# A hybrid decoder layer: where the last gate tile of the first feed-forward lies, how the norms take their root, and which engines scale the last block

## The chip, the cores and the metric

The kernel runs on one core of a Trainium2 chip. TensorE multiplies matrices (PE in the profile, its weight loads PEld), VectorE (DVE), ScalarE (ACT) and GpSimd (POOL) work on tiles in on-chip memory, SyncE (SP) issues DMA transfers. The metric is the device time of one execution in microseconds; a time stated for a kernel is the median of its runs.

## The reference

One layer of a decoder on 1024 tokens of width 1024, with 16 learned meta tokens in front, all in float32:

```
h = concat(meta, x)
u = rmsnorm(h)                    # y = x * rsqrt(mean(x*x) + 1e-6) * g
proj = u @ w_in                   # latents, queries, keys, values, indexer
A: latent attention, 8 heads:     q = rmsnorm(c_q) @ w_uq, kv = rmsnorm(c_kv) @ w_ukv, rotary part, causal softmax
B: sparse attention, 8 heads:     indexer scores, top 256 keys of each query, rotary softmax attention on them
h = h + concat(A, B) @ w_o
u = rmsnorm(h)
h = h + (silu(u @ w_gate) * (u @ w_up)) @ w_down      # hidden width 2816
out = rmsnorm(h)[16:]
```

Every norm needs, per row, the reciprocal root of a mean of squares; there are five sorts of norm: of the input, of the two latents, before the feed-forward, and at the end.

## The kernel before

Tokens are cut into eight blocks of 128 rows. Blocks 0 to 2 form part A, blocks 3 to 7 part B. In the order of the source: the input norm and projection with the indexer and the top-k search; attention of part A; the output projection of A (`out_proj`), then attention of part B, head by head, eight latent heads and eight sparse ones; the first feed-forward (`ffn`) on A; `out_proj` on B; the second feed-forward (`ffn_sums`), which forms its products from seven sums of quarter blocks; and the last norm (`last_norm`) of each block as soon as its rows are complete. Float32 factors are split into a high and a low half (`split`: ScalarE writes the high half, VectorE or GpSimd the difference, GpSimd in pieces of 256 columns), and each product is three matmuls (`three`, lines 196 to 198).

The order of the instructions on an engine isn't that of the source. The framework (a tile context) is built with `schedule_with_timeline_sim=True`: it places each instruction by its own estimate of durations when the kernel is built, so that work of later stages stands between instructions of earlier ones where memory allows. An engine then takes its queue in that fixed order. A tile's memory is given to the next tile of its name in a pool's ring when all its users are done.

The parts that matter here:

- `rstd` (L151 to L162) turns a column of sums into reciprocal roots: a scaled copy, ScalarE's root, VectorE's reciprocal, then one Newton step in four VectorE instructions (L158 to L161). The input norm calls it for nine row groups, the two latent norms 17 times together (name `rsc`), `out_proj` six times (once for three blocks of A together, once for each block of B), and `last_norm` eight times.
- `attention` (L847) keeps the split keys of a head in one of two pairs of tiles `kT`, used in turn; each holds 128 rows by the number of keys (1040 in part B). They lie in the pool `ab`. A head's scores go through an exponential on ScalarE (L799), a cast on VectorE (L819), a difference on GpSimd (L821) and a transposing DMA into `pT` (L823), then to the values' matmuls (L830 to L832).
- `ffn` (L1127) takes 22 tiles of the hidden width in turn. For each it loads a gate, an up and a down tile into `raw` (two slots in turn), and splits them with GpSimd. Gate and up tiles share a ring of two pairs (`fw`, `WF = 2`), the down tiles have another ring of two (`fu`). When it ends, its pools are closed, and the transposed rows of part B (`us`) are laid over them.
- `out_proj` on B transposes the attention's rows (L1036), writes them split into `us`, multiplies, adds the input rows, and norms each block (L1069 scales into `un`); then the block is transposed again (L1072) and its seven sums are written over `us` (`put`, L1097). The second feed-forward's first product needs the sums of all five blocks.
- `last_norm` (L1278): ScalarE squares each half of a block's rows with a running sum (L1287), the two sums are added (L1292), `rstd` follows, and each half of 512 columns is scaled by root and gain, then stored. For the blocks before the last, VectorE does the first half in one instruction (L1301), and ScalarE and GpSimd the second in two (L1298, L1299); for the last block VectorE does both halves.

Of the kernel before, what the change touches and what calls it, by code (L numbers as in the profile page):

```python
# [11 lines left out]
F32 = mybir.dt.float32  # L12
F32R = mybir.dt.float32r
# [5 lines left out]
AF = mybir.ActivationFunctionType  # L19
OP = mybir.AluOpType  # L20
# [5 lines left out]
D = 1024  # L26
P = 128
NB = T // P
# [5 lines left out]
HEADS = 8  # L34
# [5 lines left out]
NF = 2816 // P  # L40
EPS = 1e-6

NA = 3
BLK_A, BLK_B = tuple(range(NA)), tuple(range(NA, NB))
# [30 lines left out]
CH_A = (2, 2, 2)  # L75
# [5 lines left out]
WS_N, RAW_N = 5, 4  # L81
# [24 lines left out]
def hybrid_layer(ctx, tc, a, out):  # L106
    nc = tc.nc
    V, S, G, PE = nc.vector, nc.scalar, nc.gpsimd, nc.tensor
    ld = nc.sync.dma_start
# [40 lines left out]

    def rstd(pool, ss, n, parts=P, tag="rs"):  # L151

        w = ss.shape[-1]
        v = pool.tile([parts, 4, w], F32, name=tag, bufs=3)
        V.tensor_scalar(v[:, 0], ss, 1.0 / n, EPS, op0=OP.mult, op1=OP.add)
        S.activation(v[:, 1], v[:, 0], AF.Sqrt)
        V.reciprocal(v[:, 1], v[:, 1])
        V.tensor_mul(v[:, 2], v[:, 1], v[:, 1])  # L158
        V.tensor_mul(v[:, 2], v[:, 2], v[:, 0])
        V.tensor_scalar(v[:, 2], v[:, 2], -0.5, 1.5, op0=OP.mult, op1=OP.add)  # L160
        V.tensor_mul(v[:, 3], v[:, 1], v[:, 2])  # L161
        return v[:, 3]  # L162

    def v_scale(pool, i, bound, rest):
# [50 lines left out]
    def fill(n):  # L215


        while live and n > 0:
            n -= 1
            for z in list(live):  # L220
                for _ in range(z[1]):
                    if next(z[0], live) is live:
                        live.remove(z)
                        break
# [435 lines left out]
    oh = [op.tile([P, D], F32, name=f"oh{t}") for t in range(NB)]  # L660
# [186 lines left out]
    def attention(pl, blocks, cfg):  # L847
# [2 lines left out]
        cfg["b1"] = b1  # L850
        nb = len(blocks)
        nk = n_keys(b1)
        kT = cfg.get("kT") or [tuple(pl.tile([P, nk], F32R, name=f"k{x}{i}") for x in "HL") for i in range(2)]

        dma = [b for b in blocks if b not in cfg["by_pe"]]
        if dma:
# [108 lines left out]
        for i, (half, h) in enumerate(heads):  # L965
            passes, v = got.pop(i)
# [157 lines left out]
        w = -(-n // k)  # L1124
        return [(i * w, min(n, (i + 1) * w)) for i in range(k)]

    def ffn(fw, fu, blocks, u, psg, psu, pso, ch):  # L1127

        nt = len(blocks) * P
        ch, nh, nw = ch  # L1130
        hid, wdn = {}, {}
        for f in range(NF):
            ws = []
            for name in ("w_gate", "w_up", "w_down"):
                down = name == "w_down"
                pl, n = (fu, nw) if down else (fw, WF)
                raw = fw.tile([P, D], F32, name="raw", bufs=2)
                if down:
                    ld(raw, a[name][0, f * P:(f + 1) * P, :])
                else:  # L1140
                    ld(raw.rearrange("p (d c) -> p d c", c=P),
                       a[name][0, :, f * P:(f + 1) * P].rearrange("(d p) c -> p d c", p=P))
                h = pl.tile([P, D], F32R, name="wH", bufs=n)
                l = pl.tile([P, D], F32R, name="wL", bufs=n)
                split(h, l, raw, G)
                ws.append((h, l))
            wdn[f] = ws[2]
            hH = fu.tile([P, nt], F32R, name="hH", bufs=nh)
            hL = fu.tile([P, nt], F32R, name="hL", bufs=nh)
            hid[f] = hH, hL  # L1150
            for i0, i1 in block_chunks(len(blocks)):
                sl = slice(i0 * P, i1 * P)
                w = (i1 - i0) * P
                pg, pu = psg()[:, :w], psu()[:, :w]
                for o, (h, l) in ((pg, ws[0]), (pu, ws[1])):
                    for d in range(ND):
                        ds_ = slice(d * P, (d + 1) * P)
                        three(o.rearrange("p (b n) -> p b n", n=P), h[:, ds_], l[:, ds_], u[:, i0:i1, 0, d],
                              u[:, i0:i1, 1, d], d == 0, d == ND - 1)
                        if d % 2:  # L1160
                            yield
                sg = fu.tile([P, 512], F32, name="sg", bufs=1)[:, :w]

                S.activation(sg, pg, AF.Tanh, scale=0.5)
                V.scalar_tensor_tensor(sg, sg, 1.0, pg, op0=OP.add, op1=OP.mult)
                V.scalar_tensor_tensor(sg, sg, 0.5, pu, op0=OP.mult, op1=OP.mult)
                split(hH[:, sl], hL[:, sl], sg)
            if (NF - 1 - f) % ch:
                continue
            fs = range(max(0, f - ch + 1), f + 1)  # L1170
            for i, t in enumerate(blocks):
                sl = slice(i * P, (i + 1) * P)
                for c in range(2):
                    cs = slice(c * 512, (c + 1) * 512)
                    po = pso()
                    for g in fs:
                        three(po, hid[g][0][:, sl], hid[g][1][:, sl], wdn[g][0][:, cs], wdn[g][1][:, cs],
                              g == fs[0], g == fs[-1])
                    V.tensor_add(oh[t][:, cs], po, oh[t][:, cs])  # L1179
                    yield  # L1180
# [97 lines left out]
    def last_norm(fu):  # L1278

        gl = fu.tile([P, D], F32, name="gl")  # L1280
        ld(gl, bcast_rows(a["final_norm_g"], D))
        sums = {}

        def half(t, c):
            if not c:
                sums[t] = fu.tile([P, 2], F32, name="ss3", bufs=3)
            S.activation(fu.tile([P, 512], BF, name="yj"), oh[t][:, c * 512:(c + 1) * 512], AF.Square,  # L1287
                         accum_out=sums[t][:, c:c + 1])
            if not c:
                return  # L1290
            tot = fu.tile([P, 1], F32, name="ss4", bufs=3)
            V.tensor_add(tot, sums[t][:, 0:1], sums[t][:, 1:2])  # L1292
            r = rstd(fu, tot, D, P, "rs3")
            for k in range(2):
                y = oh[t][:, k * 512:(k + 1) * 512]
                g = gl[:, k * 512:(k + 1) * 512]
                if k and t < NB - 1:
                    S.activation(y, y, AF.Copy, scale=r)  # L1298
                    G.tensor_mul(y, y, g)  # L1299
                else:  # L1300
                    V.scalar_tensor_tensor(y, y, r, g, op0=OP.mult, op1=OP.mult)  # L1301
                ld(out[0, t * P:(t + 1) * P, k * 512:(k + 1) * 512], y)

        return half
# [8 lines left out]
    cfg = dict(CFG_A, s=ps_s, t=ps_t, o=ps_o, ck=(ckH, ckL), wk=(wkH, wkL), sel=selb, kT=kT_a, q_rows=q_a, v_rows=v_a)  # L1313
    woa = ExitStack()
    with aa_es:
        work = attention(aa, BLK_A, cfg)
        rest = mla_rest()
        n = 0
# [21 lines left out]
    ua = u_tile(pool(ua_es, "ua", side="right"), BLK_A, "ua")  # L1340
    ab = ExitStack()
    pl = pool(ab, "ab", side="right")
    ps_s, ps_t, ps_o, ps_g, ps_u, ps_y = (ring(x) for x in PSB)
# [16 lines left out]
    fw = pool(fa, "fw")  # L1360
    fu = pool(fa, "fua")
    for _ in work:
        fill(1)
    fill(1000)
    ab.close()
    for _ in ffn(fw, fu, BLK_A, ua, ps_g, ps_u, ps_y, CH_A):
        pass
    fa.close()
    ua_es.close()
    us = [pool(ctx, f"us{k}").tile([P, NSEG, 2, 4, SEG], F32R, name=f"us{k}") for k in range(NPR)]  # L1370
# [62 lines left out]
```

## Time and profile before

| | us |
|---|---|
| median of 3 runs | 1507.58 (1507.29 to 1510.57) |
| the profiled execution | 1510.57 |
| its span in the trace | 1508.8 |
| TensorE busy | 1403.7 (93%) |
| VectorE busy | 1101.3 (73%) |
| ScalarE busy | 923.7 (61%) |
| GpSimd busy | 893.6 (59%) |

The span runs from the first to the last instruction in the trace; the rest of an execution's time lies outside it. Busy time is the sum of an engine's instructions; matmuls are pipelined, so a busy TensorE can still be below its peak. Where a row names what ended an engine's idle time, that is inferred from the semaphores.

### The profile page before, as it was taken

How to read it: one execution, taken by the hardware profiler on the slowest of the kernel's cores; microseconds unless marked ns; L12 is line 12 of the kernel's file. 1: busy time of each engine (PE TensorE's matmuls, PEld its weight loads, DVE VectorE, ACT ScalarE, POOL GpSimd, SP SyncE). 2: the span in 40 equal slices, each digit the busy share in tenths (PEclk: the TensorE clock that was granted, in tenths of full speed). 3: DMA queues.
4: the chain of work that ended last, by engine and by line, in shares of the span. 5: the costliest groups of instructions: out<-in, count | busy, mean ns of one | idle time of the engine just before them, and what ended most of it. 6: DMA issues, size and time to landing. Idle time of an engine off the chain costs nothing. (4 is left out here: it accounts for less than half of the span.)

```text
span 1508.8 us, 29965 instructions
## 1 busy us (share of the span) xinstructions
PE 1403.7 (93%) x10320; PEld 1293.0 (86%) x10320; DVE 1101.3 (73%) x2714; ACT 923.7 (61%) x2264; POOL 893.6 (59%) x1185
## 2 busy tenths in 40 slices
PE   6999998899989799899999999897899999999996
PEld 5999998897879689798888888797899999999995
DVE  5888989948886785966776657647566777777766
ACT  5666678896888889788644444554544444444434
POOL 2573555212405587787878879663846666666653
PEclk9999999999999799999999999998899999999998
DMA  6213365223434788678879998661212222222211
GB/s 172 61 48 87 80 139 133 51 89 115 137 113 114 144 187 174 149 154 182 188 162 199 200 214 193 161 189 39 71 57 84 84 84 84 84 75 80 84 56 70
DMA packets 353737, 180.74 MB, mean 120 GB/s; under 512 B 196560, under 2 KB 341344, under 8 KB 353584
## 3 DMA queue, kind: packets, MB, share of 16 engines
q1 hardware_dynamic: 353584, 178.82, 48.0%
q8 instruction: 81, 1.33, 0.4%
q14 instruction: 72, 0.59, 0.1%
HBM read 120.77 MB, written 21.30 MB: 94 GB/s over the span
## 5 line engine op out<-in xcount | busy, mean ns | idle before, releaser
L191 POOL TENSOR_TENSOR wL<-raw,wH 128x256 fp32r<-128x256 f32 x352 | 286.7, 848 | 60.6 <-ACT wH L188 56.3
L821 POOL TENSOR_TENSOR hl<-pd,hl 128x260 f16<-128x260 f32 (+5 forms) x256 | 168.8, 689 | 70.5 <-ACT hl L817 38.0
L191 POOL TENSOR_TENSOR wsl<-raw,wsh 128x256 fp32r<-128x256 f32 x132 | 120.6, 942 | 95.9 <-ACT wsh L188 48.5
L196 PE MATMUL b<-wh,uH 128*128 128x256 f32 (+3 forms) x568 | 169.3, 298 | 5.1 <-DVE mlo L318 3.2
L198 PE MATMUL b<-wh,uL 128*128 128x256 f32 (+3 forms) x568 | 168.8, 298 | 0.0
L197 PE MATMUL b<-wl,uH 128*128 128x256 f32 (+3 forms) x568 | 168.5, 297 | 0.1
L188 ACT ACTIVATE wH<-raw 128x1024 fp32r<-128x1024 f32 x88 | 91.8, 1055 | 80.8 <-DMA raw<-in_w_gate 20.8
L196 PE MATMUL b<-us,wsh 128*128 128x320 f32 x440 | 136.2, 313 | 1.6 <-ACT us L188 1.0
L197 PE MATMUL b<-us,wsh 128*128 128x320 f32 x440 | 136.5, 311 | 0.4 <-DVE us L193 0.4
L198 PE MATMUL b<-us,wsl 128*128 128x320 f32 x440 | 134.8, 310 | 0.0
L196 PE MATMUL b<-ua,wH 128*128 128x384 f32 x352 | 121.8, 346 | 3.3 <-ACT wH L188 3.3
L382 ACT ACTIVATE js<-sc,bs 128x528 bf16<-128x528 int16 (+7 forms) x128 | 120.9, 944 | 4.8 <-DVE sc L437 2.4
L197 PE MATMUL b<-ua,wH 128*128 128x384 f32 x352 | 121.2, 344 | 0.0
L198 PE MATMUL b<-ua,wL 128*128 128x384 f32 x352 | 121.0, 345 | 0.0
L196 PE MATMUL b<-wH,hH 128*128 128x512 f32 x282 | 113.9, 404 | 4.4 <-ACT hH L188 3.1
L196 PEld LDWEIGHTS b<-wh,uH 128*128 128x128 f32 x568 | 108.8, 192 | 7.2 <-DVE mlo L318 3.9
L197 PE MATMUL b<-wL,hH 128*128 128x512 f32 x282 | 112.5, 399 | 0.0
L198 PE MATMUL b<-wH,hL 128*128 128x512 f32 x282 | 110.2, 400 | 0.4 <-DVE hL L193 0.4
L197 PEld LDWEIGHTS b<-wl,uH 128*128 128x128 f32 x568 | 109.1, 192 | 0.5 <-DVE wl L193 0.3
L198 PEld LDWEIGHTS b<-wh,uL 128*128 128x128 f32 x568 | 109.0, 192 | 0.4 <-DVE uL L193 0.2
L1248 DVE TENSOR_TENSOR oh<-b,oh 128x512 f32<-128x512 f32 x110 | 74.5, 685 | 43.3 <-PE b L198 42.6
L799 ACT ACTIVATE pd<-pd,sm 128x528 f32<-128x528 f32 (+4 forms) x80 | 75.7, 946 | 48.7 <-DVE sm L797 46.0
(410 smaller groups left out, 4834.9 us busy)
## 6 DMA issues: line engine op xcount, KB each, us to landing
raw<-in_w_gate SPq DMA_DIRECT2D x44, 512.0 KB, 4.0
raw<-in_w_up SPq DMA_DIRECT2D x44, 512.0 KB, 4.1
raw<-in_w_down SPq DMA_DIRECT2D x44, 512.0 KB, 3.6
wor<-in_w_o SPq DMA_DIRECT2D x64, 128.0 KB, 2.7
wraw<-in_w_in SPq DMA_DIRECT2D x40, 128.0 KB, 2.5
vh<-v_x SPq DMA_DIRECT2D x16, 288.0 KB, 4.0
xt<-in_x SPq DMA_DIRECT2D x8, 512.0 KB, 4.1
ks_x<-st SPq DMA_DIRECT2D x32, 128.0 KB, 2.2
```

The source lines that it names most:

```text
L188: S.activation(h, src, AF.Copy)
L191: G.tensor_sub(l[:, c], src[:, c], h[:, c])
L196: PE.matmul(o, lh, rh, start=first, stop=False, **kw)
L197: PE.matmul(o, lh, rl, start=False, stop=False, **kw)
L198: PE.matmul(o, ll, rh, start=False, stop=last, **kw)
L382: S.activation(act_junk()[:, :n_keys(b)], y[b], AF.Sign, bias=cols[0], accum_out=cnt)
L799: S.activation(pb, pb, AF.Exp, bias=mn, scale=-1.0, accum_out=z)
L821: G.tensor_sub(pl_[:, c], pb[:, c], ph[:, c])
L1248: V.tensor_add(oh[t][:, cs], po, oh[t][:, cs])
```

## The change

`rstd` takes the column times -4/n, lets ScalarE form the root of its negative, so that the reciprocal is half the wanted value, and does the Newton step in two scalar_tensor_tensor instructions where the column is one wide, in three instructions otherwise. `ffn` puts the split gate weights of its last round into `late`, the first 1024 columns of the key tiles that head 14 used; the pool `ab` is closed after `ffn`, not before. In `last_norm` the last block is multiplied by the gain into a tile `yg` (512 and 256 columns on VectorE, 256 on GpSimd) ahead of the root, and then VectorE scales its first half by the root and ScalarE its second.

```diff
 def rstd(pool, ss, n, parts=P, tag="rs"):
         v = pool.tile([parts, 4, w], F32, name=tag, bufs=3)
-        V.tensor_scalar(v[:, 0], ss, 1.0 / n, EPS, op0=OP.mult, op1=OP.add)
-        S.activation(v[:, 1], v[:, 0], AF.Sqrt)
+        V.tensor_scalar(v[:, 0], ss, -4.0 / n, -4.0 * EPS, op0=OP.mult, op1=OP.add)
+        S.activation(v[:, 1], v[:, 0], AF.Sqrt, scale=-1.0)
         V.reciprocal(v[:, 1], v[:, 1])
-        V.tensor_mul(v[:, 2], v[:, 1], v[:, 1])
-        V.tensor_mul(v[:, 2], v[:, 2], v[:, 0])
-        V.tensor_scalar(v[:, 2], v[:, 2], -0.5, 1.5, op0=OP.mult, op1=OP.add)
-        V.tensor_mul(v[:, 3], v[:, 1], v[:, 2])
+        if w == 1:
+            V.scalar_tensor_tensor(v[:, 2], v[:, 1], v[:, 1], v[:, 0], op0=OP.mult, op1=OP.mult)
+        else:
+            V.tensor_mul(v[:, 2], v[:, 1], v[:, 1])
+            V.tensor_mul(v[:, 2], v[:, 2], v[:, 0])
+        V.scalar_tensor_tensor(v[:, 3], v[:, 2], 3.0, v[:, 1], op0=OP.add, op1=OP.mult)
         return v[:, 3]
...
 def attention(pl, blocks, cfg):
-        kT = cfg.get("kT") or [...]
+        kT = cfg["kTs"] = cfg.get("kT") or [...]
...
 def ffn(fw, fu, blocks, u, psg, psu, pso, ch, late):
-                h = pl.tile([P, D], F32R, name="wH", bufs=n)
-                l = pl.tile([P, D], F32R, name="wL", bufs=n)
+                if f == NF - 1 and not ws:
+                    h, l = late
+                else:
+                    h = pl.tile([P, D], F32R, name="wH", bufs=n)
+                    l = pl.tile([P, D], F32R, name="wL", bufs=n)
                 split(h, l, raw, G)
...
 def last_norm(fu):
+            if t == NB - 1:
+                yg = fu.tile([P, D], F32, name="raw", bufs=RAW_N)
+                V.tensor_mul(yg[:, 0:512], oh[t][:, 0:512], gl[:, 0:512])
+                G.tensor_mul(yg[:, 512:768], oh[t][:, 512:768], gl[:, 512:768])
+                V.tensor_mul(yg[:, 768:], oh[t][:, 768:], gl[:, 768:])
             tot = fu.tile([P, 1], F32, name="ss4", bufs=3)
             V.tensor_add(tot, sums[t][:, 0:1], sums[t][:, 1:2])
             r = rstd(fu, tot, D, P, "rs3")
             for k in range(2):
+                if t == NB - 1:
+                    y = yg[:, k * 512:(k + 1) * 512]
+                    if k:
+                        S.activation(y, y, AF.Copy, scale=r)
+                    else:
+                        V.tensor_scalar(y, y, r, None, op0=OP.mult)
+                    ld(out[0, t * P:(t + 1) * P, k * 512:(k + 1) * 512], y)
+                    continue
                 y = oh[t][:, k * 512:(k + 1) * 512]
                 g = gl[:, k * 512:(k + 1) * 512]
-                if k and t < NB - 1:
+                if k:
                     S.activation(y, y, AF.Copy, scale=r)
                     G.tensor_mul(y, y, g)
...
     fill(1000)
-    ab.close()
-    for _ in ffn(fw, fu, BLK_A, ua, ps_g, ps_u, ps_y, CH_A):
+    late = [x[:, 0:D] for x in cfg_b["kTs"][(2 * HEADS - 2) % 2]]
+    for _ in ffn(fw, fu, BLK_A, ua, ps_g, ps_u, ps_y, CH_A, late):
         pass
+    ab.close()
     fa.close()
```

## Rows read from the trace of the kernel before

**Rows 1.** The page, part 1: busy us of each engine (share of the span) xinstructions.
```profile
PE 1403.7 (93%) x10320; PEld 1293.0 (86%) x10320; DVE 1101.3 (73%) x2714; ACT 923.7 (61%) x2264; POOL 893.6 (59%) x1185
```

**Rows 2.** Stretches: length, then busy us (count) by engine, clock, DMA share, GB/s.
```profile
100.00:200.00 100.00, 99.01 (x708) 97.54 (x707) 90.48 (x289) 68.25 (x205) 52.80 (x69) 1.00 0.35 91
...
950.00:960.00 10.00, 10.00 (x90) 9.56 (x89) 7.79 (x17) 3.31 (x6) 9.91 (x13) 1.00 0.78 185
...
960.00:980.00 20.00, 15.72 (x113) 12.44 (x112) 11.57 (x26) 10.62 (x29) 9.79 (x14) 0.91 0.66 171
...
1038.00:1060.00 22.00, 11.12 (x70) 8.95 (x69) 20.70 (x57) 10.67 (x34) 11.45 (x14) 0.70 0.09 31
```

**Rows 3.** TensorE's waits over the whole span: us in total, times, longest.
```profile
PE b L287 <- DVE xt L283: 8.9, 2, 8.4
...
PE b L314 <- ACT wh L188: 2.3, 2, 1.6
...
PE b L830 <- DMA pT<-hl: 7.1, 5, 2.4
```

**Rows 4.** Two lines' instructions: ns min/median/max, first and last start.
```profile
L158 DVE TENSOR_TENSOR rs<-rs x23: 145/159/1064, 6.4 to 1502.6; 128x1 f32<-128x1 f32 x21, 16x1 f32<-16x1 f32 x1, 128x3 f32<-128x3 f32 x1
...
L158 DVE TENSOR_TENSOR rsc<-rsc x17: 152/199/445, 110.3 to 182.1; 128x1 f32<-128x1 f32 x16, 16x1 f32<-16x1 f32 x1
...
L406 DVE SCALAR_TENSOR_TENSOR bs<-bs x64: 141/160/843, 190.2 to 631.8; 128x2 f32<-128x2 f32 x32, 128x1 f32<-128x1 f32 x32
```

**Rows 5.** VectorE in order, start of kernel: start, us, what [idle before <-releaser].
```profile
6.35 0.15 DVE L158 TENSOR_TENSOR rs<-rs 16x1 f32<-16x1 f32 x1
...
7.08 1.27 DVE L283 SCALAR_TENSOR_TENSOR xt<-xt,rs,gb 16x1024 f32<-16x1024 f32 x1
```

**Rows 6.** VectorE in order, norms of the last blocks.
```profile
1033.50 1.24 DVE L193 TENSOR_TENSOR ckL<-sc,ckH 128x512 fp32r<-128x512 f32 x1
...
1035.62 1.22 DVE L1201 TENSOR_TENSOR sc<-raw 128x512 f32<-128x512 f32 x1
...
1038.95 0.36 DVE L161 TENSOR_TENSOR rs<-rs 128x1 f32<-128x1 f32 x1
...
1047.33 0.71 DVE L161 TENSOR_TENSOR rs<-rs 128x1 f32<-128x1 f32 x1
...
1053.33 0.64 DVE L159 TENSOR_TENSOR rs<-rs 128x1 f32<-128x1 f32 x1
```

**Rows 7.** SyncE's queue, ScalarE, GpSimd and VectorE in order, the seam.
```profile
936.44 0.38 SPq L1141 DMA_DIRECT2D raw<-in_w_gate  x1
...
947.46 1.04 ACT L188 ACTIVATE wH<-raw 128x1024 fp32r<-128x1024 f32 x1
...
952.54 6.95 POOL L191 TENSOR_TENSOR wL<-raw,wH 128x256 fp32r<-128x256 f32 x8
...
953.59 0.15 DVE L797 TENSOR_SCALAR sm<-sm 128x1 f32<-128x1 f32 x1
...
954.30 1.06 ACT L188 ACTIVATE wH<-raw 128x1024 fp32r<-128x1024 f32 x1 [5.32 <-DMA raw<-in_w_up]
...
955.79 1.15 ACT L799 ACTIVATE pd<-pd,sm 128x1040 f32<-128x1040 f32 x1
...
965.76 0.60 ACT L188 ACTIVATE us<-b 128x512 fp32r<-128x512 f32 x1 [1.79 <-POOL wL L191]
```

**Rows 8.** VectorE, ScalarE and GpSimd in order, the last two blocks.
```profile
1501.32 0.16 DVE L1292 TENSOR_TENSOR ss<-ss 128x1 f32<-128x1 f32 x1
...
1501.58 0.72 ACT L1298 ACTIVATE oh<-oh,rs 128x512 f32<-128x512 f32 x1 [0.29 <-DVE rs L161]
...
1502.38 1.26 POOL L1299 TENSOR_TENSOR oh<-oh,gl 128x512 f32<-128x512 f32 x1 [1.48 <-ACT oh L1298]
...
1502.63 1.03 DVE L158 TENSOR_TENSOR rs<-rs 128x1 f32<-128x1 f32 x1
...
1504.27 1.41 DVE L1301 SCALAR_TENSOR_TENSOR oh<-oh,rs,gl 128x512 f32<-128x512 f32 x2
```

More of the change, by code (lines that the diff above doesn't have):

```diff
@@ L852, in attention @@
         nk = n_keys(b1)
-        kT = cfg.get("kT") or [tuple(pl.tile([P, nk], F32R, name=f"k{x}{i}") for x in "HL") for i in range(2)]
+        kT = cfg["kTs"] = cfg.get("kT") or [tuple(pl.tile([P, nk], F32R, name=f"k{x}{i}") for x in "HL") for i in range(2)]
         dma = [b for b in blocks if b not in cfg["by_pe"]]
@@ L1125, in block_chunks, with ffn @@
         return [(i * w, min(n, (i + 1) * w)) for i in range(k)]
-    def ffn(fw, fu, blocks, u, psg, psu, pso, ch):
+    def ffn(fw, fu, blocks, u, psg, psu, pso, ch, late):
         nt = len(blocks) * P
@@ L1364, in hybrid_layer @@
     fill(1000)
+    late = [x[:, 0:D] for x in cfg_b["kTs"][(2 * HEADS - 2) % 2]]
+    for _ in ffn(fw, fu, BLK_A, ua, ps_g, ps_u, ps_y, CH_A, late):
+        pass
     ab.close()
-    for _ in ffn(fw, fu, BLK_A, ua, ps_g, ps_u, ps_y, CH_A):
-        pass
     fa.close()
```

## The prediction

> **What bounds the kernel now.** I read the page first. TensorE is busy 93% of the span and VectorE 73% [rows 1], so what counts is where TensorE stands idle and who ends that idle time. The table of stretches prices the places that the diff touches [rows 2]: 960 to 980 us, the seam between attention, the first feed-forward and the next output projection, with 4.3 us of TensorE idle; 1038 to 1060 us, where the last blocks are normed for the second feed-forward, with 10.9 us idle, VectorE busy 20.7 of 22 us and a mean granted clock of 0.70. To these comes the end of the kernel [rows 8]. The waits of TensorE then name what ended it: at the start VectorE's scaled rows and ScalarE's split weights, in the seam a transposing DMA [rows 3]. Elsewhere matmuls that the diff leaves alone set the pace.
>
> **The norms' root.** There are 40 calls, 23 named rs and 17 rsc; 39 have one column. In those the diff drops four small VectorE instructions (L158 to L161, of which L158 stands for the four: 145 ns at least, 159 in the median, 1064 at most) for two scalar_tensor_tensors [rows 4]. The trace has none with just these operands; the nearest, L406 on one or two columns, runs from 141 to 843 ns with a median of 160 [rows 4], and I take the median. The rest only gets other constants. In a free run four of them reach from 6.35 to 7.08 us [rows 5], 0.18 us each, so a call loses 0.37 us of chain; over all calls some 15 us of VectorE's 1101 go. Most of that is hidden: the 17 rsc calls stand from 110 to 182 us [rows 4], beside a TensorE that is busy 99.0 of 100 us [rows 2]. The first output projection's call has three columns and loses one instruction; I cost that at nothing, its 0.16 us either way at most.
>
> It counts in three places.
>
> (a) The start. The first matmul waits 8.4 us for the meta row's scaled tile [rows 3], and that for L158 to L161: 0.37 us. The block after it repeats this, but there split weights are waited for as well, 2.3 us in two waits [rows 3]. Bounds: 0, if the first weights decide, and 0.75, both chains in full. I take 0.4, the one chain that TensorE is seen to wait for.
>
> (b) The norm of the last blocks, 1042 to 1060 us. VectorE's queue is nearly full, so each instruction that goes moves what lies behind it. Three calls end here with twelve of the instructions in question. Two are long beside GpSimd's work, 0.71 and 0.64 us [rows 6]; they add 1.3 us to the chain of waits, and the ten others, which follow one another or larger work at about 0.12 us, another 1.2 (an estimate from the free run's 0.18, less where the ends overlap). Half of 2.5 goes: 1.2 us. Bounds: 0.6, if both long waits move into the new instructions, and 1.9, if both vanish.
>
> (c) The end of the kernel, together with the third part below.
>
> **The gate tile.** In the last round of the first feed-forward the split gate weights go into the key buffers of head 14, free once head 15 is at work, not into the ring of two that the up weights share. So the split no longer waits for the matmuls of the gate tile before it. In the trace its load is issued at 936.44, its ScalarE half starts at 947.46 and its GpSimd half at 952.54, in a run of eight that is its own and the up tile's, 6.95 us [rows 7]. With a free target it could start near 941, some 4 us after the issue. That buys no matmul time there: TensorE is busy 10.00 of 10 us from 950 to 960 [rows 2]. The gain is later. The raw slot that this split frees takes the last down tile, and the first write into the second half's transposed rows, at 965.76, waited 1.8 us for GpSimd to end a split [rows 7], by its place the down tile's, whose raw slot lies under those rows; so out_proj's matmuls come after the stall of 2.4 us on pT [rows 3]. An earlier gate split moves the down load and this write up, and part of the stall is filled. The up tile's load uses another raw slot and comes no sooner, and the up weights now hold the ring slot that the gate weights had. I take 1.2 us, half of the stall. Upper bound 4.3, all idle time of 960 to 980. Below nothing: ScalarE takes its queue in order, and the last head's largest exp, whose bias was ready at 953.74, ran only at 955.79 [rows 7], behind the up split, which waited for its load. A gate split put ahead of an exp before its load is there does the same: 2.0 us lost. No instruction or DMA is added, and SP's queue keeps the same loads. Closing the attention's pool later costs nothing, as nothing is allocated over it until the feed-forward ends.
>
> **The last block's scaling.** Today the root waits for ScalarE, which scales another block (0.72 us, to 1502.30). After the reciprocal L158 takes 1.03 us beside GpSimd's multiply, which runs from 1502.38 to 1503.64; then come three small instructions and two scalings in series from 1504.27 to 1505.68, and the last store [rows 8]. Removed: the second scaling and two small instructions. Added: three multiplies by the gain before the norm, of 512 and 256 columns on VectorE and 256 on GpSimd; then half a scaling on VectorE and half on ScalarE. By the present scaling (0.70 each of two) VectorE's multiplies take 0.7 and 0.4 us, by half of L1299 GpSimd's takes 0.65, and ScalarE's half 0.72 as L1298 [rows 8]. VectorE's half, a tensor_scalar, has no row: between half a present scaling, 0.35, and a whole one, 0.75; either ends beside ScalarE's 0.72. If the first new instruction still waits for GpSimd until 1503.64, the second (0.18, and as much from the wait's end to its start) and ScalarE's half end near 1504.75: 0.9 us saved. Bounds: 2.0, if GpSimd's multiply is out of the way, and 0.2, if the 1.1 us of new VectorE work, which lies before the last sum in a queue that after the last matmul is nearly full, delays it by 0.7.
>
> On that wait the Trainium skill ("SBUF — State Buffer", section "SBUF: two separate sides") says that a GpSimd instruction and a VectorE one with two SBUF inputs exclude each other for the whole instruction, whichever starts second waiting. L158's 1.03 us, ended with GpSimd's multiply, agrees [rows 8]. By the rule the three new multiplies can't run side by side, which speaks against this part: GpSimd's 0.65 us would come on top of VectorE's 1.1, and the saving would be 0.25, not 0.9.
>
> **Sum.** 0.4 + 1.2 + 1.2 + 0.9 = 3.7 us. The profiled execution took 1510.57 us (span 1508.8); it is the slowest of three, the median is 1507.58. None of the terms depends on what sets them apart, so I take the sum off the median: 1503.9. The terms' bounds together give -1.2 to 9.0 us, 1498.6 to 1508.8.
>
> **Rivals.**
> *The split is hidden anyway.* The engines' order is not the source's: a weight split and a weight sum of the next stage, at 1033.50 and 1035.62, stand before the last instruction of a norm at 1038.95 [rows 6]. If the order leaves the gate's halves where they are, or the seam stays bound by attention's last chain of exp, cast, GpSimd and DMA, 2.5 us remain: 1505.1. For it: that chain ends the 2.4 us stall [rows 3]. Against: the first write waited for GpSimd's split, not for the chain.
>
> *The whole seam closes.* The exp's 2.0 us of queueing go as well, and the output projection's start fills all of the idle time, 4.3 in place of 1.2: 1498.8. Against: up tile and exp do not use the key buffers.
>
> *Slower: the freed VectorE places are filled with later work.* Weight sums and splits of the next stage already stand inside these norms [rows 6]. If the new order draws in one more set, four sums and a split at up to 1.2 us each, before the last `un`, the product that TensorE waits for comes up to 6.1 us later. With (a) and the end kept (1.3) and (b) lost: 1507.58 + 6.1 - 1.3 = 1512.4. It decides from two such instructions on, which undo the 1.3, and can be told from four on. For it: a set does stand so, and VectorE has no room (20.7 of 22 us [rows 2]). Against: the next set needs slots that GpSimd is still splitting.
>
> **How the numbers follow.** Forecast 0.50, hidden split 0.25, slower 0.17, seam closed 0.08. A difference of 0.2%, 3.0 us, is what can be told from none. Of the forecast's own range, 1498.6 to 1508.8, some three quarters lie below 1504.6: 0.38 faster, 0.12 same. Of the hidden split a quarter is faster, the rest same: 0.06 and 0.19. Seam closed: 0.08 faster. Slower: 0.16, and 0.01 same. Together faster 0.52, same 0.32, slower 0.16. The range runs from 1497.5, a little below the closed seam, to 1511.5, which leaves out the upper half of the slower case and, with a tail below, less than 2 in 10.
>
> **What would show it.** Right: the first matmul near 8.0 us; the first product on the second half's rows 1 to 2 us sooner after the last out_proj matmul; the gate split near 941 to 945 and less than 3.5 us idle in 960 to 980; the last scaling's end 0.9 us sooner after the last sum than 4.2 us (1501.48 to 1505.68). Wrong: weight sums before the last norm, an exp behind the gate split, or differences in stretches that hold no norm, where only a new order of the engines could have made them.

## The result, and the profile after

The changed kernel takes 1520.85 us (median of 4, 1519.89 to 1523.25); before, run beside it, takes 1508.95 (4 runs). The ratio is 1.0081, 95% interval 1.0060 to 1.0102: some 12 us slower, where 3.7 us less was forecast. The profiled execution took 1521.7 us, its span is 1519.9, 11.1 more than before.

The busy times hardly moved. The page, part 1, of the changed kernel [compare rows 1]:

```profile
PE 1405.8 (92%) x10320; PEld 1294.1 (85%) x10320; DVE 1097.0 (72%) x2636; ACT 927.5 (61%) x2265; POOL 888.9 (58%) x1186
```

So it isn't work that was added, but time in which TensorE stands. To find where, I took the same events from both traces. The table has them for every kernel run (one profile each, us; the runs are told of below):

| kernel | time, ratio to before (95%) | block 6's search, start of 16th pass to start of 17th | last pass, block 7 | last values' matmul ends | first feed-forward ends | first product of the second | last matmul to end of span |
|---|---|---|---|---|---|---|---|
| before | 1 | 8.7 | 741.9 | 968.1 | 977.8 | 1059.8 | 9.9 |
| changed | 1.0081 (1.0060 to 1.0102) | 21.4 | 755.8 | 984.9 | 978.9 | 1067.9 | 12.2 |
| e1 root only | 1.0053 (1.0031 to 1.0075) | 18.5 | 751.1 | 980.8 | 974.8 | 1065.3 | 9.3 |
| e2 gate tile only | 0.9987 (0.9975 to 0.9999) | 8.9 | 739.7 | 966.3 | 972.5 | 1057.7 | 9.9 |
| e3 scaling only | 1.0013 (0.9998 to 1.0027) | 8.9 | 736.7 | 960.7 | 970.5 | 1053.8 | 10.9 |
| e4 gate and scaling | 0.9996 (0.9979 to 1.0014) | 9.0 | 740.2 | 965.5 | 973.3 | 1056.0 | 11.4 |
| e5 changed, hinge on VectorE | 0.9990 (0.9972 to 1.0009) | 7.5 | 751.1 | 977.4 | 983.6 | 1063.6 | 12.2 |
| e6 before, hinge on VectorE | 1.0080 (1.0048 to 1.0112) | 8.2 | 742.9 | 970.4 | 981.2 | 1068.9 | 9.8 |
| e7 changed, 3 passes fewer | 0.9949 (0.9924 to 0.9973) | 17.7 | 732.4 | 960.1 | 968.1 | 1047.9 | 11.5 |
| e8 before, 3 passes fewer | 1.0001 (0.9984 to 1.0018) | 8.9 | 725.1 | 948.7 | 973.9 | 1055.6 | 9.8 |
| e9 before, 3 passes more | 1.0089 (1.0074 to 1.0104) | 8.9 | 758.3 | 987.9 | 972.7 | 1073.8 | 9.9 |
| e10 root, gate, hinge | 0.9984 (0.9967 to 1.0001) | 6.7 | 745.5 | 972.9 | 979.1 | 1060.2 | 9.3 |
| e11 block 6 on VectorE | 1.0115 (1.0100 to 1.0130) | | | 995.4 | 996.9 | 1081.3 | 9.6 |
| e12 scaling without GpSimd | 0.9988 (0.9976 to 1.0000) | 8.7 | 736.4 | 962.1 | 970.5 | 1054.1 | 10.8 |
| e13 as e10, half the gain ahead | 0.9972 (0.9958 to 0.9987) | 7.0 | 743.9 | 969.1 | 975.4 | 1056.8 | 9.9 |
| e14 the kernel of e10, more rounds | 0.9974 (0.9954 to 0.9994) | 7.9 | 749.9 | 976.8 | 983.1 | 1062.5 | 9.3 |

For before and after: 8.1 of the 11.1 us are lost by the first product of the second feed-forward, 0.7 within it, 2.3 after the last matmul.

A row is one execution, and executions of one order of the instructions differ too. Before, e3 and e12 have the same order until the last norm; their last pass of block 7 starts 736.4 to 741.9, their last values' matmul ends 960.7 to 968.1. In e5, e10, e13 and e14, which also share an order until the last norm, it is 743.9 to 751.1 and 969.1 to 977.4. So a difference of a few us between two single rows shows nothing by itself.

**What is late.** The sparse heads need the best 256 keys of each row. A bisection finds them, pass by pass: ScalarE counts the scores over a threshold (a Sign with a running sum, L382 before, L385 after) and forms the next threshold. Blocks 6 and 7 go through ScalarE one after the other, 32 passes each, the upper 16 bits first. Between the halves of a block stands a hinge: two small GpSimd steps (L389 and L390, after L392 and L393), then a count and a scalar_tensor_tensor on VectorE (L436 and L437, after L439 and L440). It is a chain beside the attention of the latent heads, and the diff doesn't touch it. Block 6's hinge in the kernel before, ScalarE, GpSimd and VectorE in order (start, us, what [idle before <-releaser]):

```profile
510.02 1.05 ACT L382 ACTIVATE js<-sc,bs 128x912 bf16<-128x912 int16 x1
...
512.92 0.29 ACT L383 ACTIVATE bs<-bs,th 128x1 f32<-128x1 f32 x1
...
513.60 0.20 POOL L390 TENSOR_TENSOR bs<-bs 128x1 f32<-128x1 f32 x1
...
513.87 1.15 DVE L436 TENSOR_SCALAR_CACHE_REDUCE jk<-sc,bs 128x912 bf16<-128x912 int16 x1
...
514.96 1.48 DVE L437 SCALAR_TENSOR_TENSOR sc<-sc,bs 128x912 uint16<-128x912 int16 x1
...
518.71 1.04 ACT L382 ACTIVATE js<-sc,bs 128x912 bf16<-128x912 uint16 x1
```

The same hinge in the changed kernel:

```profile
513.69 1.05 ACT L385 ACTIVATE js<-sc,bs 128x912 bf16<-128x912 int16 x1
...
517.57 0.28 ACT L386 ACTIVATE bs<-bs,th 128x1 f32<-128x1 f32 x1
...
517.74 2.80 POOL L194 TENSOR_TENSOR wL<-raw,wH 128x256 fp32r<-128x256 f32 x4
520.50 0.23 POOL L392 TENSOR_SCALAR bs<-bs 128x1 f32<-128x1 f32 x1
520.68 2.80 POOL L194 TENSOR_TENSOR wL<-raw,wH 128x256 fp32r<-128x256 f32 x4
523.44 1.80 POOL L824 TENSOR_TENSOR hl<-pd,hl 128x228 f16<-128x228 f32 x3
525.18 0.21 POOL L393 TENSOR_TENSOR bs<-bs 128x1 f32<-128x1 f32 x1
525.33 3.20 POOL L824 TENSOR_TENSOR hl<-pd,hl 128x228 f16<-128x228 f32 x5
528.47 5.59 POOL L194 TENSOR_TENSOR wL<-raw,wH 128x256 fp32r<-128x256 f32 x8
...
526.55 0.29 DVE L196 TENSOR_TENSOR qL<-b,qH 96x128 fp32r<-96x128 f32 x1 [4.50 <-ACT qH L191]
526.76 1.15 DVE L439 TENSOR_SCALAR_CACHE_REDUCE jk<-sc,bs 128x912 bf16<-128x912 int16 x1
...
527.84 7.19 DVE L440 SCALAR_TENSOR_TENSOR sc<-sc,bs 128x912 uint16<-128x912 int16 x1
...
535.06 1.06 ACT L385 ACTIVATE js<-sc,bs 128x912 bf16<-128x912 uint16 x1 [5.29 <-DVE sc L440]
```

From the 16th pass to the 17th it takes 21.4 us in place of 8.7. The new order of the queues has put the two GpSimd steps behind splits: from L386's start to L393's end 7.8 us, 0.9 before. It has put the VectorE steps behind qL, which waits 4.50 us for its high half, most of it beside the GpSimd steps: L439 starts 1.4 us after L393's end. And L440, the same instruction on the same shape, takes 7.19 us in place of 1.48, with GpSimd at work beside it both times (this part differs from run to run, see the end).

Block 7's hinge is hit too. Its 16th and 17th pass before:

```profile
660.75 1.16 ACT L382 ACTIVATE js<-sc,bs 128x1040 bf16<-128x1040 int16 x1
...
667.26 1.16 ACT L382 ACTIVATE js<-sc,bs 128x1040 bf16<-128x1040 uint16 x1 [1.17 <-DVE sc L437]
```

and after, with the GpSimd step that ends late:

```profile
679.87 1.15 ACT L385 ACTIVATE js<-sc,bs 128x1040 bf16<-128x1040 int16 x1
...
686.78 5.61 POOL L194 TENSOR_TENSOR wL<-raw,wH 128x256 fp32r<-128x256 f32 x8
692.33 0.20 POOL L393 TENSOR_TENSOR bs<-bs 128x1 f32<-128x1 f32 x1
...
700.07 1.17 ACT L385 ACTIVATE js<-sc,bs 128x1040 bf16<-128x1040 uint16 x1 [2.94 <-DVE sc L440]
```

That is 20.2 us in place of 6.5. The search starts at the same time in both kernels (445.6 and 445.7). The changed one is 3.7 us behind at block 6's 16th pass, 16.4 at its 17th and 32.8 at block 7's 17th. The 15 passes after that take 55.7 us, before 74.6: the chain had some slack there, and 13.9 us are left at block 7's last pass. The last pass of block 7 and the first sparse head's exponential on it, before:

```profile
741.90 1.16 ACT L382 ACTIVATE js<-sc,bs 128x1040 bf16<-128x1040 uint16 x1
...
768.23 1.15 ACT L799 ACTIVATE pd<-pd,sm 128x1040 f32<-128x1040 f32 x1
```

and after:

```profile
755.75 1.15 ACT L385 ACTIVATE js<-sc,bs 128x1040 bf16<-128x1040 uint16 x1
...
785.15 1.06 ACT L191 ACTIVATE wH<-raw 128x1024 fp32r<-128x1024 f32 x1 [6.05 <-DMA raw<-in_w_up]
786.12 1.15 ACT L802 ACTIVATE pd<-pd,sm 128x1040 f32<-128x1040 f32 x1
```

The exponential is 17.9 us late, 4 us more than the pass. Its bias is ready at 780.37, but a weight split stands ahead of it in ScalarE's queue and waits for its load, so it starts 5.8 us after the bias; before it was 2.1.

The latent heads are in time (their last exponential on block 7 starts at 713.3, before at 718.7); the sparse heads run 17 us behind to their end. The first feed-forward, whose matmuls fill TensorE beside attention, keeps its time. Before, it ends 9.7 us after the last values' matmul; after, 6.0 us ahead of it, and for the end of attention no filling is left. TensorE's stretches in the kernel before (columns as in rows 2):

```profile
760.00:800.00 40.00, 37.51 (x271) 33.84 (x270) 26.69 (x69) 17.34 (x37) 31.11 (x44) 1.00 0.78 170
...
980.00:1000.00 20.00, 19.26 (x161) 19.07 (x162) 15.98 (x35) 12.39 (x33) 16.11 (x18) 1.00 0.84 254
```

and in the changed one:

```profile
760.00:800.00 40.00, 34.01 (x187) 28.91 (x185) 26.66 (x50) 11.98 (x19) 28.09 (x31) 0.96 0.42 110
...
960.00:980.00 20.00, 18.21 (x168) 15.58 (x165) 16.00 (x42) 7.29 (x16) 13.12 (x19) 1.00 0.53 91
980.00:1000.00 20.00, 15.54 (x124) 14.12 (x123) 13.27 (x29) 14.92 (x39) 8.29 (x10) 0.87 0.81 210
```

From 760 to 800, where the sparse heads start, 6.0 us are idle in place of 2.5, and the seam's idle time has moved from 960 to 980 [rows 2] to the stretch after it, where the mean granted clock is 0.87 in place of 1.00. TensorE also waits 5.3 us at 288 us for a small tile of VectorE's (`vw`, L171), 0.3 us before; as the search starts no later, that is not what makes it late, and what it costs is open.

### The profile page after: what moved, and what is told of

Read it like the earlier page. It is cut to its first block, busy times and chain, and to the rows that moved or that the text cites. A ratio compares the mean times of both kernels' runs of the same rounds, so it can differ in the third digit from the quotient of the medians.

```text
span 1519.9 us, 29882 instructions
## 1 busy us (share of the span) xinstructions
PE 1405.8 (92%) x10320; PEld 1294.1 (85%) x10320; DVE 1097.0 (72%) x2636; ACT 927.5 (61%) x2265; POOL 888.9 (58%) x1186
## 4 chain that ended last, share of the span: by engine, by line
PE 42%; DVE 17%; DMA 10%; POOL 8%; ACT 7%; issue 6%; SPq 0%; POOLq 0%; DVEq 0%; ACTq 0%
PE b L199 12%; PE b L201 12%; PE b L200 12%; DMA pT<-hl 4%; POOL wL L194 4%; DVE jk L400 3%; POOL hl L824 2%; PE b L793 2%; DMA raw<-in_w_gate 1%; ACT js L385 1%; DMA raw<-in_w_up 1%; DVE pd L795 1%; DMA raw<-in_w_down 1%; DVE bs L409 1%; ACT pd L802 1%
## 5 line engine op out<-in xcount | busy, mean ns | idle before, releaser
L194 POOL TENSOR_TENSOR wL<-raw,wH 128x256 fp32r<-128x256 f32 x348 | 283.1, 847 | 63.5 <-ACT wH L191 59.8
L385 ACT ACTIVATE js<-sc,bs 128x528 bf16<-128x528 int16 (+7 forms) x128 | 121.0, 946 | 14.8 <-DVE sc L440 10.4
L199 PE MATMUL b<-ua,wH 128*128 128x384 f32 x344 | 118.6, 345 | 0.6 <-ACT wH L191 0.6
L200 PE MATMUL b<-ua,wH 128*128 128x384 f32 x344 | 118.5, 345 | 0.0
L1255 DVE TENSOR_TENSOR oh<-b,oh 128x512 f32<-128x512 f32 x110 | 74.6, 685 | 43.7 <-PE b L201 43.0
```

The costliest lines, as they stand in the source:

```text
L194: G.tensor_sub(l[:, c], src[:, c], h[:, c])
L199: PE.matmul(o, lh, rh, start=first, stop=False, **kw)
L200: PE.matmul(o, lh, rl, start=False, stop=False, **kw)
L385: S.activation(act_junk()[:, :n_keys(b)], y[b], AF.Sign, bias=cols[0], accum_out=cnt)
```

## The experiments

The theory tested: the new root makes the planned order put block 6's hinge late, and the late selection is the loss. Rivals: the gate tile's new order (B); VectorE's freed places in the norms (C); the order of later stages, with the late search a bystander (D).

**The parts by themselves.** e1 has only the new root, e2 only the gate tile's part, e3 only the new scaling in `last_norm`, e4 the last two.

> The new root alone; gate tile and last scaling as before. Theory A (the shorter root lets the engines' order be planned anew: the step between the halves of block 6's threshold search, L436 to L438, falls behind other splits and beside GpSimd's back-to-back work, and every later selection is some 12 us late): slower than the kernel before by 10 to 15 us, and the first pass of the second half of that search starts near 535 us in place of 518.7. Rival B (the gate tile's part re-plans the first feed-forward and second attention and costs it): within 2 us of before. Rival C (VectorE's freed places in the norms of the last blocks are filled with later work): up to 5 us slower, all of it between 1033 and 1060 us, and the search as before.

> The gate tile in the key buffers alone; old root, old scaling. Theory A: within 2 us of before, the first pass of block 6's second half starts within 3 us of 518.7. Rival B: slower by 8 to 15 us, with the stall in the same search or after 940 us.

> The last block's scaling alone. The order of all engines is that of before until the last stage, so the difference is the tail's: by the prediction's term 0.9 us faster; by the tail seen in the changed kernel (last scaling's end 8.0 us after the last matmul, 6.8 before) 1.2 us slower. Theories A and B expect no more than this.

> Gate tile and last scaling with the old root (the change without its first part). Theory A: within 3 us of before, so some 10 to 14 us faster than the changed kernel. Rival B: slower by 8 to 15 us, as the changed kernel. Rival C: as theory A, but the new root alone then costs at most 5 us.

Measured: root alone 8.0 us slower (ratio times 1510), with the late hinge (the 17th pass at 530.0); gate tile alone 2.0 us faster, scaling alone 2.0 us slower (its interval just crosses 1), both together no difference, all three with the hinge in time. Root alone thus costs less than the 10 to 15 us expected (its interval is 4.7 to 11.3). Its queues have the changed kernel's order until some 935 us, and both hinges are late in it, 18.5 and 20.2 us. Since e4 is level with before, it is the root that brings the loss, and the root only shortens calls and so changes the planned order. Rival B falls. Rival C falls too: the norms got faster (below). The parts add up to 8.0 us, the whole has 12.2; the intervals overlap.

**The hinge put right.**

```diff
-                G.tensor_scalar(up, up, 0.5, None, op0=OP.mult)
-                G.tensor_sub(cols[1], up, cols[0])
+                V.tensor_scalar(up, up, 0.5, None, op0=OP.mult)
+                V.tensor_sub(cols[1], up, cols[0])
```

> The changed kernel with the two one-column steps between the halves of the search (L392, L393) on VectorE in place of GpSimd, so that they no longer stand behind GpSimd's splits; the planned order then puts L439 and L440 ahead of both qL halves, as the kernel before has them. Theory A (the delay between the halves of block 6's search, handed on by every later pass, is what costs): the first pass of the second half starts before 523 us (535.1 in the changed kernel), the search of block 7 ends near 745 (755.8), and the time is 1506 to 1512, 8 to 14 us under the changed kernel. Rival D (the slow stretch is after 760 us, in attention and feed-forward as newly ordered, and the search only happens to be late): the search gets faster, but the time stays within 4 us of 1520.9.

> The kernel before with the same two steps on VectorE: the control. They hardly waited there (0.4 us on GpSimd). Theory A: within 3 us of before, as far as the first pass of the second half stays within 3 us of 518.7; if it is later, the time is later by about as much. Rival D: within 3 us whatever the search does.

With this edit the changed kernel falls to 1507.86 us, level with before. But the edit doesn't act alone: the order of the queues is another one from 220 us on. Block 6's hinge, VectorE and ScalarE in order (the profiled execution, 1515.42 us, is the slowest of e5's ten):

```profile
517.26 0.15 DVE L392 TENSOR_SCALAR bs<-bs 128x1 f32<-128x1 f32 x1 [1.44 <-ACT bs L386]
517.45 0.42 DVE L393 TENSOR_TENSOR bs<-bs 128x1 f32<-128x1 f32 x1
517.90 1.16 DVE L439 TENSOR_SCALAR_CACHE_REDUCE jk<-sc,bs 128x912 bf16<-128x912 int16 x1
...
518.99 1.19 DVE L440 SCALAR_TENSOR_TENSOR sc<-sc,bs 128x912 uint16<-128x912 int16 x1
...
520.55 1.05 ACT L385 ACTIVATE js<-sc,bs 128x912 bf16<-128x912 uint16 x1
```

Nothing waits there now. At block 7's hinge the moved step itself is held:

```profile
672.08 8.32 DVE L393 TENSOR_TENSOR bs<-bs 128x1 f32<-128x1 f32 x1
```

So that hinge takes 13.7 us (20.2 in the changed kernel), and the search ends at 751.1, not near 745. The time is in theory A's range and out of rival D's. But in e1, which is 8.0 us slower than before, the search ends at 751.1 as well. The end of the search alone doesn't decide; whether attention then ends after the first feed-forward does go with the loss (see below).

The control did not go as expected: e6 is some 12 us slower than before (1.0080). Its 17th pass is 6.5 us later, for which theory A allowed about as much, yet its search ends within 1 us of before's and attention within 2.3. In its one profile (1517.14 us, under its median of 1521.64) most of the loss comes after: from the end of the first feed-forward to the first normed block's transposition 58.6 us, before 52.9. So a new order can lose as much at another place, which I have not followed further. The same edit gains some 14 us in one order and loses 12 in the other, so e5 does not show that block 6's hinge alone was what cost.

**The search by itself.** Only block 6's second half is changed in the source (the comments here name the runs); the order of the queues differs from some 550 us on:

```diff
-                for k in range(15, -1, -1):
+                for k in range(12 if first and b == 6 else 15, -1, -1):   # e7, e8
+                for k in [15, 14, 13, 12] + 3 * [12] * (first > 0 and b == 6) + list(range(11, -1, -1)):   # e9
```

> The changed kernel without three of the sixteen passes of the second half of block 6's search (so another threshold is chosen; nothing else is left out). The delay between the halves stays. Three passes take 13 us there. Theory A: the search of block 7 ends some 10 to 13 us earlier, near 744, and the time falls by 8 to 13 us, to about 1510. Rival D: the time falls by the passes' own work alone, 3 x 1.2 us of ScalarE that is not the bound: 1518 to 1521.

> The kernel before without the same three passes of block 6. Theory A in its strong form (the selection of block 7 sets when the sparse heads start, in this kernel too): faster by 5 to 13 us. In its weak form (before, TensorE has other work until the selection is there, and only the late search of the changed kernel passes that point): within 3 us. Rival D: within 3 us.

> The kernel before with three more passes in the second half of block 6's search (another threshold is chosen); the order up to there is that of before. It gives the kernel before a search that ends late, as the changed kernel has, with none of the change in it. Theory A, weak form (what counts is that the sparse heads wait for block 7's selection): the search of block 7 ends near 755 in place of 741.9, and the time is 6 to 14 us above before. Rival D (the lateness of the search is harmless, the loss comes from the order of later stages): within 3 us of before.

This tells most. In the kernel before, three passes fewer change nothing (1.0001), though the last pass comes 16.8 us earlier. Three more cost 13.4 us (1.0089), as much as the whole change, with none of it in the kernel; the last pass comes 16.4 us later (block 7's hinge takes 17.4 us there, in place of 6.5, which the edit did not aim at). Last pass and first sparse exponential of e9:

```profile
758.27 1.15 ACT L382 ACTIVATE js<-sc,bs 128x1040 bf16<-128x1040 uint16 x1
...
787.21 1.17 ACT L799 ACTIVATE pd<-pd,sm 128x1040 f32<-128x1040 f32 x1 [0.58 <-DVE sm L797]
```

They stand within 3 us of the changed kernel's. In the changed kernel three passes fewer give back some 20 us (1.0081 to 0.9949), more than the 8 to 13 expected. The last pass comes 23.4 us earlier there, not 10 to 13: in e7's order block 7's hinge, which the edit leaves alone, takes 7.2 us in place of 20.2.

Theory A holds in its weak form, and rival D as stated falls. The table shows what the slow kernels with a late search share: in the changed kernel, e1 and e9 the last values' matmul ends 6.0, 6.0 and 15.3 us after the first feed-forward, in all others ahead of it (in e11 by 1.5). One rival is left: these edits give the rest of the queues a new order too, a new order can cost 12 us with the search in time (e6), and no run moves the search with the rest as it was. So that the root's new order costs 8.0 us is measured; that the late selection is the whole of it is argued from these runs, not shown.

**Versions.** e10 and e14 are one kernel: the change without its new scaling, with the hinge on VectorE. e11 is the change without its new scaling, the hinge on GpSimd, and deals the searches out otherwise:

```diff
-TOPK_B = [([[5]], False, 2), ([[6], [7]], True, 3)]
+TOPK_B = [([[5], [6]], False, 2), ([[7]], True, 3)]
```

e12 is e3 with `V.tensor_mul` for `G.tensor_mul` in `yg`. e13 is e5 with

```diff
-                V.tensor_mul(yg[:, 0:512], oh[t][:, 0:512], gl[:, 0:512])
-                G.tensor_mul(yg[:, 512:768], oh[t][:, 512:768], gl[:, 512:768])
-                V.tensor_mul(yg[:, 768:], oh[t][:, 768:], gl[:, 768:])
+                V.tensor_mul(yg[:, 512:], oh[t][:, 512:], gl[:, 512:])
...
-                        V.tensor_scalar(y, y, r, None, op0=OP.mult)
+                        V.scalar_tensor_tensor(y, oh[t][:, 0:512], r, gl[:, 0:512], op0=OP.mult, op1=OP.mult)
```

> New root and gate tile, the two steps between the search's halves on VectorE, the last scaling as before. Theory A together with theory T (the new scaling of the last block costs about 1.9 us at the end, by the spans after the last matmul: 9.2 to 9.9 us in four kernels without it, 10.9 to 12.2 in five with it): 2 us faster than the same kernel with the new scaling, 1504 to 1507, that is 1 to 4 us faster than before; span after the last matmul under 10 us. If the tail's spread is chance: 1506 to 1510.

> New root and gate tile, the old scaling, and the searches dealt out otherwise: VectorE searches blocks 5 and then 6, ScalarE only block 7, so that both end earlier. Theory A: with the selection some 15 us earlier than in the changed kernel the sparse heads don't wait, and the time is 1500 to 1508. If VectorE, which is 78% busy in that stretch, can't take the 32 passes more (32 x 1.2 us), its splits and maxima for the latent heads are late, and the time is 1512 to 1525.

> The last block's new scaling alone, with GpSimd's 256 columns of the multiply by the gain on VectorE. Theory T1 (the tail is lost because GpSimd's and VectorE's multiplies hold each other up, and hold up the small root instructions): the span after the last matmul is 9.9 us or less, 0.5 to 1.5 us under the 10.9 of the scaling with GpSimd's piece. Theory T2 (the loss is the two stores on SP's queue behind each other and one more, and the two small instructions beside the other block's GpSimd multiply): it stays at 10.5 to 11.3 us.

> New root, gate tile, the search's two steps on VectorE, and a third form of the last scaling: only the second 512 columns are multiplied by the gain ahead of the root (one VectorE instruction of 0.68 us, nothing on GpSimd); after the root VectorE scales and multiplies its half in one instruction, ScalarE scales the other. Theory T1 (the new scaling loses by its 1.5 us of multiplies on VectorE ahead of the last sum and by GpSimd's piece, while its end after the sum is 0.7 us shorter): span after the last matmul 9.2 to 10.0 us, time 0 to 1 us under the same kernel with the old scaling. Theory T2 (the loss is in the holds of the small root instructions by other blocks' GpSimd multiplies and in the stores' order, whatever multiplies there are): 10.4 to 11.4 us, time 1 to 2 us over it.

> New root, gate tile and the search's two steps on VectorE with the old scaling, timed beside e13 on one chip and against before in more rounds. Theory A with T: faster than before by 2 to 4 us (ratio 0.9975 to 0.999), the interval clear of 1; span after the last matmul 9.2 to 10.0 us. If the gain seen so far is the spread of single profiles: ratio 1.000 with an interval across 1.

e13 and e14 beat both kernels: 0.9972 and 0.9974, some 4 us under before, both intervals clear of 1; e10 pointed there. e11 is 17 us slower: VectorE is busy 59.25 of the 60 us from 700 to 760 (before 46.83), so the second expectation came, its time just above the range (1526.25). e12 is mixed: its time is 1.8 us under before (e3's 2.0 over it, on another chip), its span after the last matmul 10.8 us, as T2 had it. e13's 9.9 is in T1's range. In it, with one multiply ahead of the sum, the sum ends 3.0 us after the last matmul, in e10 and e14 with none 3.3, in e5 with three (one of them GpSimd's) 4.6, but in e3 with the same three 2.7. So the multiplies delay the sum in one order and not in the other; how much of that is GpSimd's piece isn't settled.

## Why the prediction was wrong

**The step that failed** is "Elsewhere matmuls that the diff leaves alone set the pace", and with it the costing of the hidden rsc calls at nothing. That a call beside a busy TensorE takes less time costs nothing at its own place, but it changes the estimate from which the order of everything after it is planned. The root alone made the kernel 8.0 us slower (e1). In the new order the two hinges of the search take 18.5 and 20.2 us, before 8.7 and 6.5, the sparse heads start late, and attention ends 6.0 us after the feed-forward whose matmuls fill its gaps; before, it ends 9.7 us ahead of that. Which of the 40 calls turns the order was not tested. The prediction saw new orders as a risk in the norms and in the seam, and never asked which chain elsewhere a new order could break. The search was in the profile: 64 Sign passes on blocks 6 and 7, 4.3 to 5.0 us from pass to pass on average, with ScalarE, GpSimd and VectorE in the chain, and the sparse heads at its end. The slower rival got the sign for a reason that didn't come: its place, 1033 to 1060, became faster, and its 1512.4 is 8.5 us short. The last sentence on what would show it wrong, differences in stretches that hold no norm, is what came.

**The start (0.4).** Not seen. The first scaling starts 0.17 us sooner [rows 5], and waits for another input:

```profile
6.91 1.27 DVE L286 SCALAR_TENSOR_TENSOR xt<-xt,rs,gb 16x1024 f32<-16x1024 f32 x1 [0.37 <-DMA gb<-in_attn_norm_g]
```

TensorE's first wait is 8.2 us, 8.4 before [rows 3], and 7.9 to 8.9 in other kernels with the new root. The first new instruction is longer than the row that I took for it (160 ns): line L160 after, ns min/median/max:

```profile
L160 DVE SCALAR_TENSOR_TENSOR rs<-rs x22: 205/220/1217, 6.2 to 1513.5; 128x1 f32<-128x1 f32 x21, 16x1 f32<-16x1 f32 x1
```

**The last blocks' norms (1.2).** Right. From the first transposition of normed rows to the first product of the second feed-forward it takes 29.1 us before (1030.7 to 1059.8) and 27.6 after (1040.3 to 1067.9): 1.5 us. Each of the seven other kernels with the new root has 27.6 there, each of the seven others with the old one 29.1. A next-stage weight sum does stand inside such a norm (L1206 at 1047.48, between L160 and L164), without harm.

**The gate tile (1.2).** Right in direction, 2.0 us by e2 (0.2 to 3.8). There the split starts 4.1 us after the issue of its load, as foreseen, before 11.0 [rows 7]:

```profile
934.33 0.40 SPq L1142 DMA_DIRECT2D raw<-in_w_gate  x1
...
938.41 1.06 ACT L188 ACTIVATE kH<-raw 128x1024 fp32r<-128x1024 f32 x1 [1.45 <-DMA raw<-in_w_gate]
```

The stall on pT shrinks as foreseen: 1.4 us in e2 and 1.8 in e4, 2.4 before and in e3 and e12. But a wait of 2.1 and 1.7 us for VectorE (L1056) comes in behind it, so that TensorE's waits from 940 to 1000 add up to 5.1 us in e2 as before; where the 2.0 us come from the single profiles don't show. In the changed kernel attention's lateness holds the split, as the keys are still in use:

```profile
945.45 1.06 ACT L191 ACTIVATE kH<-raw 128x1024 fp32r<-128x1024 f32 x1 [2.87 <-PE b L793]
```

**The last block's scaling (0.9).** Wrong sign. Its end in parts (us, one profile each):

| kernel | last matmul to the end of the last sum | from there to the last scaling's end | from there to the span's end |
|---|---|---|---|
| before | 2.6 | 4.2 | 3.1 |
| e1 root alone (e10 and e14 the same) | 3.3 | 2.9 | 3.1 |
| e3 scaling alone | 2.7 | 4.7 | 3.5 |
| e12 scaling alone, no GpSimd piece | 2.4 | 4.9 | 3.5 |
| changed | 4.6 | 3.5 | 4.2 |

In the changed kernel the part behind the last sum is 0.75 shorter than before (3.45 us, 1512.31 to 1515.76), close to the 0.9. That is luck: the root alone saves 1.3 there, and the new scaling adds some 0.5 with either root. What was also mis-sized is the bound of 0.7 on the delay of the sum: it is 2.0 us here, 1.3 over the root alone. The multiplies stand in VectorE's queue ahead of the sum, and GpSimd's, with another block's behind it, holds the sum up. With the old root (e3, e12) the sum isn't late. VectorE, GpSimd, ScalarE and the stores' queue in order, after [rows 8]:

```profile
1510.31 0.87 DVE L1303 TENSOR_TENSOR raw<-oh,gl 128x256 f32<-128x256 f32 x1
1511.10 1.21 DVE L1305 TENSOR_TENSOR ss<-ss 128x1 f32<-128x1 f32 x1
...
1513.53 1.22 DVE L160 SCALAR_TENSOR_TENSOR rs<-rs 128x1 f32<-128x1 f32 x1
...
1509.80 1.10 POOL L1302 TENSOR_TENSOR raw<-oh,gl 128x256 f32<-128x256 f32 x1 [2.88 <-DVE oh L1255]
1510.86 1.44 POOL L1320 TENSOR_TENSOR oh<-oh,gl 128x512 f32<-128x512 f32 x1
1513.47 1.26 POOL L1320 TENSOR_TENSOR oh<-oh,gl 128x512 f32<-128x512 f32 x1 [1.17 <-ACT oh L1319]
...
1515.04 0.72 ACT L1311 ACTIVATE raw<-raw,rs 128x512 f32<-128x512 f32 x1 [1.64 <-DVE rs L164]
...
1515.92 0.38 SPq L1323 DMA_DIRECT2D out_y<-oh  x1
1516.39 0.40 SPq L1314 DMA_DIRECT2D out_y<-raw  x1
```

L1305 adds two columns and takes 1.21 us, to the end of GpSimd's L1320. Then the last store stands behind another block's in SP's queue and is issued 0.6 us after its data are there; the span ends 4.2 us after the last scaling, 3.1 before. The kernels with this scaling have 10.9 to 12.2 us after the last matmul, those with the old 9.3 to 9.9: 2.0 us between the means, the difference that e3's time has (its own profile has 1.0).

**The sum.** Norms 1.5 and gate tile 2.0 are of the size of what e13 and e14 bring (some 4 us), but one profile each doesn't apportion it: e14's reaches the first product of the second feed-forward 2.7 us later than before's, and makes up 4.9 us within that stage. Against the gains stand the new order, some 14 us between the ratios of the changed kernel and e5, and the tail.

## What to carry to other kernels

Where the order of the queues is planned from estimated durations, a shorter instruction anywhere is a change of order everywhere after it: look for the longest serial chain through several engines, read from the trace how much slack it has, and see where a long run of another engine's work can stand ahead of its hand-overs. Moving a hand-over to another engine is no cure by itself: it plans the order anew, and GpSimd's run held the moved step for 8.32 us. Test a part by itself before its terms are added up. Work taken off the very end can come to stand ahead of the sum that the end waits for.

## What the runs showed of the hardware

A VectorE instruction with two inputs in on-chip memory, block 6's scalar_tensor_tensor at the hinge (128x912), ran beside a gapless run of GpSimd's pieces in the kernels before and after, e1 to e3, e5 and e7. It took 1.16 to 1.61 us in all kernels but two, 3.00 in e1 and 7.19 in the changed kernel; in e7, where the queues stand there as in those two, 1.18. So with one order of the queues around it the instruction was held in some executions and not in others. The Trainium skill ("SBUF — State Buffer", section "SBUF: two separate sides") has GpSimd and such an instruction exclude each other for the whole instruction. A wait for one of GpSimd's pieces agrees with the short cases (a piece takes 0.64 us of 3.20 for five, or 0.70 of 5.59 for eight), but the 7.19 were a wait for several pieces in a row: it ended 1.0 us after the run of eight. In e1's and e7's profiles the 17th pass is late all the same, 18.5 and 17.7 us after the 16th: at this hinge the place in the queues costs most of the delay, the hold the rest.

The longest hold fell on a one-column instruction. L393 at block 7's hinge, on VectorE in e5, e10, e13 and e14, took 8.32, 8.32, 8.33 and 8.32 us; at the other hinges of these kernels it took 0.15 to 0.51. In all four it ended within 0.02 us of the end of a gapless run of GpSimd's pieces, 12 of which had started after it.
